# One more buffer for high halves, a gather of unsplit tokens, and the transposition of up behind both down products, in a two-layer decoder kernel

## Chip, cores, metric

One core of a Trainium2 chip runs the whole kernel. The metric is the device time of the kernel in microseconds; the kernel before takes 1362.1 us (median of three runs, 1359.48 to 1362.96).

## What is computed

A decoder trunk of two layers over 256 tokens of 1024 channels in float32. Layer 0 mixes by pooling and sliding-window attention, then a dense SwiGLU; layer 1 mixes by dilated attention and a short convolution, then a SwiGLU of eight experts, of which each token uses two. The change touches the last part:

```python
def swiglu(x, w_gate, w_up, w_down):
    return (jax.nn.silu(x @ w_gate) * (x @ w_up)) @ w_down

def moe_swiglu(x, w_router, w_gate, w_up, w_down):
    top_logit, top_e = lax.top_k((xt @ w_router).astype(jnp.float32), TOP_K)   # 2 of 8
    gates = jax.nn.softmax(top_logit, axis=-1)
    ...
    def expert_block(args):
        xb, e = args
        return (jax.nn.silu(xb @ w_gate[e]) * (xb @ w_up[e])) @ w_down[e]
    ...                                   # gather rows by expert, run, add back by gate

# every sub-layer: x = layer_norm(ALPHA * x + f(x)); expert hidden width 3584
```

## The kernel before

**Weights.** All weights come as one stream of pieces of 1 MB (128 partitions x 2048 float32), loaded by the queue of SyncE (SP) into raw buffers as these come free. Most products are made from float32 split in two: a high half `wh`, cast by ScalarE (ACT, `hi`, L258), and a low half `wl`, what is left after taking `wh` from the raw piece, by VectorE (DVE, `lo`, L275); `lo` then gives the raw buffer back, and with that the next load starts. `wh` has a ring of four tiles, `wl` one of three. When TensorE (PE) has used a piece, `drop` (L301) calls `pump` (L282), which lets ScalarE cast a piece if it is at most two ahead of the piece in use, and VectorE subtract one if it is at most one ahead.

**Experts.** Each expert's hidden width of 3584 is cut into seven chunks of 512. A step (`step`, L1407) does one chunk of one expert: two pieces of gate, two of up, and then the two down pieces of the chunk of the step before it. There are 56 steps. An expert with many tokens is heavy (H): its products take three split matmuls each (`mm3`, L316 to L318), and the two down pieces of most heavy chunks are used raw, as native float32 (L1224). An expert with at most 64 tokens is light (T): it holds the high and low halves of its tokens side by side in 128 columns, so two split matmuls do (`mm2`, L1226 with `wh`, L1227 with `wl`), and the two halves of the result in `h` are transposed and folded together: `fold_of` (L1234) gives four transposes on PE (L1237), a copy of one half on ScalarE (L1240) and an addition of the other on VectorE (L1241). That is done for gate (`sg`) and for up (`us`); afterwards VectorE multiplies them (L1466), ScalarE casts the high half `hh` of the product (L1467), and VectorE subtracts the low one (L1468). `h` is copied from PSUM by ScalarE for gate (L1427) and for up (L1439). The sequence of H and T, by `mixed`, is mostly "heavy, light, light", with some "heavy, light".

**Tokens.** Before an expert starts, its tokens are gathered by products with one-hot matrices (`Unit`, L1161). For that the normalized tokens `x` are split once into `xkh` and `xkl`; `gather` (L1176) multiplies either half, and the copies out of PSUM (`half` L1185, `thin` L1190) go to ScalarE but one. Expert outputs are added into `x` (L1285).

**Order.** The program is written under a manual schedule: each engine runs its instructions in the order in which the code issues them. So the order of `pump`, copies, folds and gathers on ScalarE and VectorE is that of the calls in `step`.

Of the kernel before, what the change touches and what calls it, by code (L numbers as in the profile page):

```python
# [10 lines left out]
F32 = mybir.dt.float32  # L11
F32R = mybir.dt.float32r
# [75 lines left out]
def trunk(ctx, tc, stream, x_tok, x_t, pos, ln_w, ln_b, pool_bd, pool_sc, sinks, conv_w, router, cf, cb, windows,  # L88
# [20 lines left out]
    def bank():  # L109
        return rings.next("bank") if "bank" in rings.at else ps1.tile([128, 512], F32, name="bank")  # L110
# [16 lines left out]
    def split(hi, lo, src):  # L127
        nc.scalar.copy(hi, src)
        nc.vector.tensor_sub(lo, src, hi.bitcast(F32))
# [23 lines left out]
    class Weights:  # L153
        def __init__(self):
            self.order = []
            self.native, self.base = set(), [0]
            self.raw, self.split, self.loaded = {}, {}, 0
            self.free = [raw1.tile([128, PIECE], F32, name=f"raw{i}") for i in range(RAW1)]
            self.kept = {}
            self.limit = LIMIT  # L160
            self.taken = self.used = 0
            self.at_hi = self.at_lo = (0, 0)
# [118 lines left out]

        def pump(self, n=1, full=False):  # L282
            for _ in range(n):
                self.hi(AHEAD if full else AHEAD - 1)
                k = self.at_lo[0]
                if k - self.used < AHEAD - 1 if k >= MOE_BASE else self.step(self.at_lo) != self.at_hi:
                    self.lo()
# [599 lines left out]
    with tc.tile_pool(name="od1", bufs=1) as e1, tc.tile_pool(name="od2", bufs=2) as e2:  # L887
# [151 lines left out]
    identb = cbf[:, B_ID:B_TRI]  # L1039
    early.close()  # L1040
    raw3 = ctx.enter_context(tc.tile_pool(name="raw3", bufs=1))
    xk, yb = [raw2.tile([128, PIECE], F32R, name=f"xk{i}") for i in range(2)], \
        raw2.tile([128, PIECE], F32R, name="yb")
    raws = [raw3.tile([128, PIECE], F32, name=f"raw{RAW1 + i}") for i in range(RAW2 + RAW3 - 3)]
    lasting = raws[:3]
    W.give_back(*raws)
    mm, na, nb, oa, ob = proj_out(wb, lambda: None)
    ctx.enter_context(tc.manual_schedule())
    xkh, xkl = [t.rearrange("p (i d) -> p i d", i=2) for t in xk]
    lgp = bank()  # L1050
    lg0 = lgp[:, :2 * NE].rearrange("p (i e) -> p i e", e=NE)

    def route(norm, c):
# [8 lines left out]
            for k in range(2):  # L1062
                nc.tensor.matmul(lg0[:, i], xt[:, k], rw[:, c + k], start=c + k == 0, stop=c + k == KC - 1)
        return logits

    def split_tokens(i):
        split(xkh[:, i], xkl[:, i], x[:, i])

    na.add(1, oa[1])
    na.finish()  # L1070
# [15 lines left out]
    W.drop(0)  # L1086
    lga()
    lga = route(na, 4)
    nc.scalar.copy(xkh[:, 0], x[:, 0])
    lgb()  # L1090
    nc.vector.tensor_sub(xkl[:, 0], x[:, 0], xkh[:, 0].bitcast(F32))
    lgb = route(na, 6)
    W.lo()
    mm(ob, 3, 1)
# [17 lines left out]
    lga()  # L1112
    lgb()
    keep(KEEP[2])
    nc.scalar.copy(xkh[:, 1], x[:, 1])
    W.hi()
    W.hi()

# [42 lines left out]
    class Unit:  # L1161
# [11 lines left out]
            for i in range(2):  # L1173
                self.one_hot(self.oh[:, i], iota[:, :self.oh.shape[2]], i)

        def gather(self, a, c, b, m):  # L1176
            for k in range(c, c + 512 // m):
                for i in range(2):
                    nc.tensor.matmul(b[:, (k - c) * m:(k - c + 1) * m],  # L1179
                                     (xkh, xkl)[a][:, i, k * 128:(k + 1) * 128],  # L1180
                                     self.oh[:, i], start=i == 0, stop=i == 1)

        def half(self, c, a, b, copy):
            self.gather(a, c, b, 128)
            copy(self.xg[a][:, c:c + 4], b.rearrange("p (k s) -> p k s", s=128))  # L1185

        def thin(self, a):
            b = bank()
            self.gather(a, 0, b, LIGHT)
            nc.scalar.copy(self.xg[0][:, :, a * LIGHT:(a + 1) * LIGHT], b.rearrange("p (k s) -> p k s", s=LIGHT))  # L1190

        def parts(self):
            yield self.start()
            for j in range(2 if self.light else 4):
                if self.light:
                    self.thin(j)
                else:
                    self.half(4 * (j % 2), j // 2, bank(), nc.vector.tensor_copy if j == 3 else nc.scalar.copy)
                yield

        def aim(self):
            ohb = rings.tiles["ohb"][0]
# [86 lines left out]
    nc.vector.tensor_copy(cnt, psb[:, 16:24])  # L1289
    ln2.close()  # L1290
    m2 = ctx.enter_context(tc.tile_pool(name="mo2", bufs=1, side="right"))
    rings.add("oh", [m2.tile([128, 2, 128], F32R, name="oh")])
    rings.add("ohb", [m2.tile([128, 2, 128], F32R, name="ohb")])
    rings.add("oht", [m2.tile([128, 2, 128], F32R, name="oht")])
    rings.add("h", [m2.tile([128, 512], F32, name="h")])
# [5 lines left out]
    accs = [acc() for _ in range(4)]  # L1301
    rings.add("bank", [bank() for _ in range(4)])
    places = [big_tile(t) for t in ("mh", "ml")]
    unit = Unit(places[0], 0, False, slot)
    unit.start()
    nc.vector.tensor_sub(xkl[:, 1], x[:, 1], xkh[:, 1].bitcast(F32))
    W.lo()
    for c in (0, 4):
        unit.half(c, 0, acc(), nc.scalar.copy)
    for c in (0, 4):  # L1310
        unit.half(c, 1, bank(), nc.vector.tensor_copy if c == 0 else nc.scalar.copy)
    for _ in range(4):
        W.hi()
    W.lo()
# [4 lines left out]
    def gates():  # L1319
        nc.vector.tensor_scalar(gt[:, 0], gt[:, 1], 1.0, None, op0=OP.add)  # L1320
        nc.vector.reciprocal(gt[:, 0], gt[:, 0])
        nc.vector.tensor_mul(gt[:, 1], gt[:, 1], gt[:, 0])
        nc.vector.tensor_mul(gate, hots[0], bc(gt[:, 0]))
        nc.vector.tensor_mul(hots[1], hots[1], bc(gt[:, 1]))
        nc.vector.tensor_add(gate, gate, hots[1])
        nc.scalar.activation(x, x, AF.Copy, scale=ALPHA)

    def sort_experts():
        rank = cst[:, C_RANK:C_INV]
# [39 lines left out]
    class Experts:  # L1369
# [37 lines left out]
        def step(self, s):  # L1407
            nonlocal aux, ones_row, rows, wb
            p, n = self.seq[s]
            unit, left = self.units[p], len(self.seq) - 1 - s  # L1410
            light = unit.light
            self.part(p)
            ended = self.units[self.prev[0]] if self.prev is not None and self.prev[1] == NCH - 1 else None
            if ended or left == 0:
                (ended or unit).aim()

            def proj(b, j):
                (half_light if light else half_proj)(b, W.take(512), j, *unit.xg)
# [12 lines left out]
            up = bank()  # L1431
            proj(up, 0)
            if light:
                sg, us = rings.next("sg"), rings.next("us")
                fold_of(sg, h)()
                nc.scalar.activation(sg, sg, AF.Silu)
            proj(up, 1)
            if light:
                nc.scalar.copy(h, up)  # L1439
            else:  # L1440
                nc.vector.tensor_mul(h, h, up)
            self.part()
            if left < 4:
                spread(*divmod(3 - left, 2))
            if self.prev is not None:
                pe, pn, pht = self.prev
                if pn == 0:
                    self.begin(pe)
                finish(down_half(self.y[pe], pht, 0, pn, W.take(None)))
                W.drop()  # L1450
            if light:
                fold_up = fold_of(us, h)
            if left == 0:
                unit.back()
            if self.prev is not None:
                finish(down_half(self.y[pe], pht, 1, pn, W.take(None)))
                W.drop()
                if ended:
                    split_y(yb[:, :D], yb[:, D:], self.y.pop(pe))
                    ended.back()  # L1460
                    self.todo = combine_of(pe, ended.oht)
            if light:
                ht = rings.next("hh")
                s3 = sg.rearrange("p (k t) -> p k t", t=LIGHT)
                fold_up()
                nc.vector.tensor_mul(sg, sg, us)  # L1466
                nc.scalar.copy(ht[:, :, :LIGHT], s3)  # L1467
                self.late = lambda: nc.vector.tensor_sub(ht[:, :, LIGHT:], s3, ht[:, :, :LIGHT].bitcast(F32))  # L1468
                self.prev = (p, n, (ht,))
            else:  # L1470
                self.prev = (p, n, flip_h(h, (p, n, 4) in self.native))
            if s >= FIXED:
                self.follow(p, n)
            if left == 6:
                aux = W.borrow(0)
                ones_row = aux[:1, :128]
                nc.vector.memset(ones_row, 1.0)
                rows = W.borrow(1)[:1].rearrange("p (a d) -> p a d", a=2)
                for a, src in enumerate((ln_w, ln_b)):
                    nc.sync.dma_start(rows[:, a], src[1, 1][None, :])  # L1480
                wb = W.borrow(2).rearrange("p (a d) -> p a d", a=2)
            if left == 9:
                W.hold(*lasting)
# [23 lines left out]
    def tail(x8):  # L1507
# [2 lines left out]
        x8.settle()  # L1510
        spare = bank()
        for _ in range(7):
            nc.tensor.matmul(spare, xkh[:, 0, :128], xkh[:, 0, :512], start=True, stop=True)
        e, n, ht = x8.prev
        y, oht = x8.y[e], x8.units[e].oht

# [205 lines left out]
```

## Time and profile before

| | |
|---|---|
| median of three runs | 1362.1 us (1359.48 to 1362.96) |
| the profiled execution, its own time | 1365.56 us |
| its span in the trace | 1363.8 us, at a granted TensorE clock of 0.99 |
| busy in the span | PE 97%, weight loads 78%, VectorE 80%, ScalarE 67%, GpSimd 0% |
| HBM traffic | 424.88 MB read, 1.05 MB written |

The profiled execution is 3.5 us longer than the median; the rows below are of that one. Times in the trace are microseconds from the span's start. The first 475 us or so hold layer 0 and the mixer and router of layer 1, the rest is the expert part with a tail of some 20 us. In a row of the trace "x8" counts records; a native float32 matmul leaves two records, and the listing of instructions below counts it once.

### The profile page before, as it was taken

Reading aid. Unit: us, or ns where it says so; the run is one execution under the profiler, and the core shown is the slowest. Engines: PE = TensorE matmul, PEld = TensorE weight load, DVE = VectorE, ACT = ScalarE, POOL = GpSimd, SP = SyncE. Lnnn points to the kernel's source line nnn. Section 1 sums busy time; section 2 is a strip of 40 time slices with the busy share of each in tenths; the row PEclk is TensorE's granted clock in tenths of the full one; section 3 lists DMA queues with packets and bytes.
Section 4 is the critical chain, followed back from the end, with each engine's and each line's share of the span. In section 5 each row is a group of like instructions: output and inputs, shape, how many; then the busy total and the mean of one; then the engine's idle time right before and its main releaser. Section 6 shows DMA issues by size and latency. Waiting matters only on the chain. (4 is left out here: it accounts for less than half of the span.)

```text
span 1363.8 us, 18760 instructions
## 1 busy us (share of the span) xinstructions
PE 1321.2 (97%) x6944; PEld 1069.5 (78%) x6944; DVE 1084.4 (80%) x1110; ACT 917.3 (67%) x1026; POOL 2.5 (0%) x8
## 2 busy tenths in 40 slices
PE   8999999999999989999999999999999999999995
PEld 6888999988999778877777777787777877777764
DVE  6866555587655688899898899898889979988987
ACT  5735444455544477788776788778678769776883
POOL 0000000000000000000000000000000000000000
PEclk9999999999999999999999999999999999999998
DMA  8617655535424689999999999999999999999991
GB/s 261 234 62 222 205 187 186 187 124 186 155 78 149 261 307 370 346 417 401 420 387 362 377 420 420 418 419 419 419 392 419 419 405 419 420 419 350 418 411 41
DMA packets 72375, 426.61 MB, mean 313 GB/s; under 512 B 8914, under 2 KB 9682, under 8 KB 30548
## 3 DMA queue, kind: packets, MB, share of 16 engines
q1 hardware_dynamic: 71412, 424.32, 79.9%
q0 software_dynamic: 576, 0.62, 0.3%
q8 instruction: 56, 0.92, 0.3%
q10 hardware_dynamic: 288, 0.39, 0.1%
q14 instruction: 43, 0.35, 0.1%
HBM read 424.88 MB, written 1.05 MB: 312 GB/s over the span
## 5 line engine op out<-in xcount | busy, mean ns | idle before, releaser
L275 DVE TENSOR_TENSOR wl<-raw,wh 128x2048 fp32r<-128x2048 f32 (+2 forms) x435 | 823.6, 1914 | 155.6 <-ACT wh L258 126.9
L258 ACT CAST wh<-raw 128x2048 fp32r<-128x2048 f32 (+2 forms) x437 | 695.0, 1607 | 140.1 <-PE bank L318 62.8
L1226 PE MATMUL bank<-wh,ml 128*128 128x512 f32 x536 | 220.5, 411 | 1.1 <-ACT h L1427 1.1
L1227 PE MATMUL bank<-wl,ml 128*128 128x512 f32 x536 | 211.5, 395 | 0.9 <-DVE wl L275 0.6
L318 PE MATMUL bank<-wl,mh 128*128 128x512 f32 x336 | 131.8, 392 | 3.1 <-DVE wl L275 3.1
L316 PE MATMUL bank<-wh,mh 128*128 128x512 f32 x336 | 134.0, 399 | 0.0
L317 PE MATMUL bank<-wh,mh 128*128 128x512 f32 x336 | 131.4, 391 | 0.4 <-ACT mh L1185 0.4
L1227 PEld LDWEIGHTS bank<-wl,ml 128*128 128x128 f32 x536 | 100.8, 188 | 28.5 <-DVE wl L275 6.1
L1226 PEld LDWEIGHTS bank<-wh,ml 128*128 128x128 f32 x536 | 100.8, 188 | 22.6 <-issue 3.1
L316 PE MATMUL bank<-xth,wh 128*128 128x256 f32 x416 | 118.1, 284 | 0.0
L317 PE MATMUL bank<-xth,wl 128*128 128x256 f32 x416 | 117.7, 283 | 0.0
L318 PE MATMUL bank<-xtl,wh 128*128 128x256 f32 x416 | 117.7, 283 | 0.0
L1226 PE MATMUL acc<-wh,hh 128*128 128x512 f32 (+1 forms) x308 | 115.3, 381 | 0.8 <-DVE hh L1468 0.8
L1224 PE MATMUL acc<-raw,hf 128*128 128x512 f32 x256 | 115.2, 593 | 0.0
L1227 PE MATMUL acc<-wl,hh 128*128 128x512 f32 (+1 forms) x308 | 112.9, 373 | 0.0
L1224 PEld LDWEIGHTS acc<-raw,hf 128*128 128x128 f32 x256 | 47.1, 190 | 47.1 <-issue 46.0
L316 PEld LDWEIGHTS bank<-xth,wh 128*128 128x128 f32 x416 | 79.8, 192 | 0.4
L317 PEld LDWEIGHTS bank<-xth,wl 128*128 128x128 f32 x416 | 79.8, 192 | 0.4
L318 PEld LDWEIGHTS bank<-xtl,wh 128*128 128x128 f32 x416 | 79.8, 192 | 0.0
L318 PEld LDWEIGHTS bank<-wl,mh 128*128 128x128 f32 x336 | 63.5, 189 | 16.9 <-DVE wl L275 3.5
L317 PEld LDWEIGHTS bank<-wh,mh 128*128 128x128 f32 x336 | 63.5, 189 | 14.6 <-issue 1.0
L316 PEld LDWEIGHTS bank<-wh,mh 128*128 128x128 f32 x336 | 63.5, 189 | 13.8 <-issue 1.0
(284 smaller groups left out, 1849.0 us busy)
## 6 DMA issues: line engine op xcount, KB each, us to landing
raw<-in_stream SPq DMA_DIRECT2D x326, 1024.0 KB, 9.8
raw<-in_stream SPq DMA_DIRECT2D x142, 512.0 KB, 4.9
ln_wb<-in_ln_w SPq DMA_DIRECT2D x3, 512.0 KB, 8.1
ln_wb<-in_ln_b SPq DMA_DIRECT2D x3, 512.0 KB, 9.5
xraw<-in_x_t SPq DMA_DIRECT2D x4, 256.0 KB, 7.2
raw<-in_stream SPq DMA_DIRECT2D x4, 256.0 KB, 5.0
x<-in_x_tok SPq DMA_DIRECT2D x1, 1024.0 KB, 7.0
win<-in_windows SPq DMA_DIRECT2D x1, 768.0 KB, 10.9
```

Of the source, the lines that this page charges most:

```text
L258: nc.scalar.copy(self.split[k][0][:, c], self.raw[k][:, c])
L275: nc.vector.tensor_sub(wl[:, c], self.raw[k][:, c], wh[:, c].bitcast(F32))
L316: nc.tensor.matmul(o, ah, bh, start=start, stop=False)
L317: nc.tensor.matmul(o, al, bh, start=False, stop=False)
L318: nc.tensor.matmul(o, ah, bl, start=False, stop=stop)
L1224: nc.tensor.matmul(o, a if a.dtype == F32 else a.bitcast(F32), bh, start=start, stop=stop)
L1226: nc.tensor.matmul(o, a, bh, start=start, stop=False)
L1227: nc.tensor.matmul(o, a, bl, start=False, stop=stop)
```

## The change

It has three parts.

1. The ring of `wh` gets a fifth tile, and from then on `pump` lets ScalarE cast up to three pieces ahead of the one in use (`W.deep = AHEAD`), where it was two. The rule for `lo` is as before.
2. The tokens are no longer split. `x` stays as `tokens`, sums go into a new tile `xsum`, the one-hot matrix is float32, and `gather` multiplies the unsplit tokens by native matmuls: 16 per unit where there were 32. The result is split out of PSUM by `split`: ScalarE casts the high half, VectorE subtracts.
3. `fold_of(us, h)`, the transposition of up and its copy, is called behind both down halves instead of between them.

```diff
@@ pump
-                self.hi(AHEAD if full else AHEAD - 1)
+                self.hi(AHEAD if full else self.deep)
@@ after the early pools are closed
-    xk, yb = [raw2.tile([128, PIECE], F32R, name=f"xk{i}") for i in range(2)], \
-        raw2.tile([128, PIECE], F32R, name="yb")
+    xsum = raw2.tile([128, 2, D], F32, name="xsum")
+    yb = raw2.tile([128, PIECE], F32R, name="yb")
+    rings.tiles["wh"].append(raw2.tile([128, PIECE], F32R, name=f"wh{AHEAD + 1}"))
+    W.deep = AHEAD
...
-    nc.scalar.copy(xkh[:, 0], x[:, 0])
-    nc.vector.tensor_sub(xkl[:, 0], x[:, 0], xkh[:, 0].bitcast(F32))
...
@@ Unit
-        def gather(self, a, c, b, m):
-            for k in range(c, c + 512 // m):
+        def gather(self, c, b):
+            m = LIGHT if self.light else 128
+            for k in range(512 // m):
                 for i in range(2):
-                    nc.tensor.matmul(b[:, (k - c) * m:(k - c + 1) * m],
-                                     (xkh, xkl)[a][:, i, k * 128:(k + 1) * 128],
+                    nc.tensor.matmul(b[:, k * m:(k + 1) * m], tokens[:, i, (c + k) * 128:(c + k + 1) * 128],
                                      self.oh[:, i], start=i == 0, stop=i == 1)
...
+            hi, lo = [t[:, c:c + 512 // m] for t in self.xg] if not self.light else \
+                     [self.xg[0][:, :, a * m:(a + 1) * m] for a in range(2)]
+            split(hi, lo, b.rearrange("p (k s) -> p k s", s=m))
...
@@ before the experts
+    tokens, x = x, xsum
...
-        nc.scalar.activation(x, x, AF.Copy, scale=ALPHA)
+        nc.scalar.activation(x, tokens, AF.Copy, scale=ALPHA)
@@ step
                 finish(down_half(self.y[pe], pht, 0, pn, W.take(None)))
                 W.drop()
-            if light:
-                fold_up = fold_of(us, h)
             if left == 0:
                 unit.back()
             if self.prev is not None:
                 finish(down_half(self.y[pe], pht, 1, pn, W.take(None)))
                 W.drop()
...
             if light:
+                fold_up = fold_of(us, h)
                 ht = rings.next("hh")
                 s3 = sg.rearrange("p (k t) -> p k t", t=LIGHT)
                 fold_up()
```

The change moves lines: L1224 becomes L1209, L1226 and L1227 become L1211 and L1212, L1237, L1240 and L1241 become L1222, L1225 and L1226; L1427, L1439, L1466 and L1467 become L1410, L1422, L1448 and L1449.

How PE's rows change in a light step behind a heavy one, in the stretch from the end of up to the next gate (`hf` is the heavy chunk's product, `ml` the tokens of the light expert). Before:

```order
L1226 MATMUL bank<-wh_80,ml 128x512
L1227 MATMUL bank<-wl_84,ml 128x512
L1224 MATMUL acc<-raw_4332,hf 128x512 x4
L1237 MATMUL bank<-cst,h 128x128 x4
L1224 MATMUL acc<-raw_4333,hf 128x512 x4
L1226 MATMUL bank<-wh_81,ml 128x512
L1227 MATMUL bank<-wl_85,ml 128x512
```

Now:

```order
L1211 MATMUL bank<-wh_80,ml 128x512
L1212 MATMUL bank<-wl_84,ml 128x512
L1209 MATMUL acc<-raw_4332,hf 128x512 x4
L1209 MATMUL acc<-raw_4333,hf 128x512 x4
L1222 MATMUL bank<-cst,h 128x128 x4
L1211 MATMUL bank<-wh_81,ml 128x512
L1212 MATMUL bank<-wl_85,ml 128x512
```

The four transposes of `h` have gone from between the two native down halves to behind the second.

ScalarE's rows for the same step, from the copy of the heavy product (`hf`) to the cast of the light product (`hh`). Before:

```order
L1249 COPY hf<-bank 128x512
L258 CAST wh_80<-raw_4330 128x2048
L1427 COPY h<-bank 128x512
L1240 COPY sg<-bank 128x256
L1436 ACTIVATE sg<-sg 128x256
L258 CAST wh_81<-raw_4331 128x2048
L1439 COPY h<-bank 128x512
L258 CAST wh_82<-raw_4335 128x2048
L1240 COPY us<-bank 128x256
L258 CAST wh_79<-raw_4336 128x2048
L1467 CAST hh<-sg 128x4x64
```

Now:

```order
L1234 COPY hf<-bank 128x512
L1410 COPY h<-bank 128x512
L258 CAST wh_81<-raw_4331 128x2048
L1225 COPY sg<-bank 128x256
L1419 ACTIVATE sg<-sg 128x256
L258 CAST wh_82<-raw_4335 128x2048
L1422 COPY h<-bank 128x512
L258 CAST wh_4329<-raw_4336 128x2048
L258 CAST wh_79<-raw_87 128x2048
L1225 COPY us<-bank 128x256
L1449 CAST hh<-sg 128x4x64
```

Each cast of a piece stands about one place earlier against the copies of `h` and the folds, and the copy of `us` stands directly ahead of `hh`.

VectorE's rows in the like step of an earlier expert, from the fold of gate (`sg`) to the low half of the light product. Before:

```order
L1241 TENSOR_TENSOR sg<-sg,bank 128x256
L275 TENSOR_TENSOR wl_85<-raw,wh_79 128x2048
L275 TENSOR_TENSOR wl_83<-raw_4330,wh_80 128x2048
L1241 TENSOR_TENSOR us<-us,bank 128x256
L1466 TENSOR_TENSOR sg<-sg,us 128x256
L1169 TENSOR_SCALAR ohb<-iota,hot_4610 128x128 x2
L275 TENSOR_TENSOR wl_84<-raw_4332,wh_81 128x2048
L1468 TENSOR_TENSOR hh<-sg,hh 128x4x64
```

Now:

```order
L1226 TENSOR_TENSOR sg<-sg,bank 128x256
L275 TENSOR_TENSOR wl_85<-raw,wh_79 128x2048
L275 TENSOR_TENSOR wl_83<-raw_4330,wh_80 128x2048
L1226 TENSOR_TENSOR us<-us,bank 128x256
L1448 TENSOR_TENSOR sg<-sg,us 128x256
L1164 TENSOR_SCALAR ohb<-iota,hot_4607 128x128 x2
L275 TENSOR_TENSOR wl_84<-raw_4332,wh_81 128x2048
L1450 TENSOR_TENSOR hh<-sg,hh 128x4x64
```

VectorE's order is the same before and now.

## Rows read from the trace of the kernel before

**Rows 1.** The page: busy time, and DMA in 40 slices (tenths).

```profile
PE 1321.2 (97%) x6944; PEld 1069.5 (78%) x6944; DVE 1084.4 (80%) x1110; ACT 917.3 (67%) x1026; POOL 2.5 (0%) x8
...
DMA  8617655535424689999999999999999999999991
```

**Rows 2.** Busy time by stretch: engines' busy us (instructions), PE clock, DMA share, GB/s.

```profile
740.00:1220.00 480.00, 478.16 (x2086) 361.43 (x2085) 426.22 (x295) 377.74 (x329) 0.00 (x0) 1.00 1.00 413
```

**Rows 3.** Waits, 580 to 1340 us: us in total, times, longest us.

```profile
DVE wl L275 <- ACT wh L258: 40.8, 27, 2.3
...
PE bank L1237 <- ACT h L1439: 2.8, 4, 1.4
...
PE bank L1227 <- DVE wl L275: 0.6, 2, 0.3
...
PEld bank L1227 <- DVE wl L275: 6.1, 15, 0.7
```

**Rows 4.** Timeline of VectorE, 1128 to 1177: start, us, what [idle before, releaser].

```profile
1131.21 0.41 DVE L1241 TENSOR_TENSOR us<-us,bank 128x256 f32<-128x256 f32 x1
...
1156.92 8.89 DVE L275 TENSOR_TENSOR wl<-raw,wh 128x2048 fp32r<-128x2048 f32 x4
1166.44 0.42 DVE L1241 TENSOR_TENSOR sg<-sg,bank 128x256 f32<-128x256 f32 x1 [0.64 <-ACT sg L1240]
1169.13 4.58 DVE L275 TENSOR_TENSOR wl<-raw,wh 128x2048 fp32r<-128x2048 f32 x2 [2.27 <-ACT wh L258]
1173.63 0.41 DVE L1241 TENSOR_TENSOR us<-us,bank 128x256 f32<-128x256 f32 x1
```

**Rows 5.** Timeline of PE, 1161 to 1180.

```profile
1163.12 0.39 PE L1227 MATMUL bank<-wl,ml 128*128 128x512 f32 x1
1163.35 0.39 PE L1226 MATMUL bank<-wh,ml 128*128 128x512 f32 x1
1163.66 0.50 PE L1227 MATMUL bank<-wl,ml 128*128 128x512 f32 x1
...
1167.68 3.60 PE L1224 MATMUL acc<-raw,hf 128*128 128x512 f32 x8
1171.12 0.60 PE L1237 MATMUL bank<-cst,h 128*128 128x128 f32 x4
1171.55 3.60 PE L1224 MATMUL acc<-raw,hf 128*128 128x512 f32 x8
1174.59 0.80 PE L1226 MATMUL bank<-wh,ml 128*128 128x512 f32 x1
```

**Rows 6.** Timeline of ScalarE, 1161 to 1177.

```profile
1166.03 0.37 ACT L1240 COPY sg<-bank 128x256 f32<-128x256 f32 x1 [1.89 <-PE bank L1237]
...
1171.75 0.37 ACT L1240 COPY us<-bank 128x256 f32<-128x256 f32 x1 [0.37 <-PE bank L1237]
```

**Rows 7.** Busy time in the cycle of one heavy and two light steps.

```profile
1131.21:1163.60 32.39, 32.32 (x145) 25.70 (x143) 32.17 (x23) 28.01 (x24) 0.00 (x0) 1.00 1.01 420
...
1131.21:1173.63 42.42, 42.35 (x181) 31.89 (x180) 39.29 (x27) 35.29 (x31) 0.00 (x0) 1.00 1.01 420
```

**Rows 8.** Timeline of VectorE, 634 to 668 and, in a heavy step, 850 to 884.

```profile
636.00 0.41 DVE L1241 TENSOR_TENSOR us<-us,bank 128x256 f32<-128x256 f32 x1
...
856.56 2.29 DVE L275 TENSOR_TENSOR wl<-raw,wh 128x2048 fp32r<-128x2048 f32 x1 [0.95 <-issue]
```

**Rows 9.** Gathers and native matmuls: timelines of PE, and L129 by line (count, busy us, mean ns).

```profile
585.65 1.87 PE L1179 MATMUL bank<-oh,xk 128*128 128x64 f32 x16
...
416.26 1.00 PE L1013 MATMUL bank<-v,pt 128*128 128x64 f32 x8
...
L129 DVE TENSOR_TENSOR yb<-acc,yb 128x512 fp32r<-128x512 f32 x14 | 9.3, 687 | 7.6 <-ACT yb L128 7.6
```

**Rows 10.** Timelines of VectorE and PE at the first gather.

```profile
470.55 1.22 DVE L1306 TENSOR_TENSOR xk<-x,xk 128x1024 fp32r<-128x1024 f32 x1
...
470.54 2.10 PE L1179 MATMUL acc<-oh,xk 128*128 128x128 f32 x16 [0.69 <-PE bank L1151]
```

More of the change, by code (lines that the diff above doesn't have):

```diff
@@ L158, in __init__ @@
             self.free = [raw1.tile([128, PIECE], F32, name=f"raw{i}") for i in range(RAW1)]
[L159 removed]
+            self.kept, self.deep = {}, AHEAD - 1
             self.limit = LIMIT
@@ L1048, in trunk @@
     ctx.enter_context(tc.manual_schedule())
-    xkh, xkl = [t.rearrange("p (i d) -> p i d", i=2) for t in xk]
     lgp = bank()
@@ L1064, in route @@
         return logits
-    def split_tokens(i):
-        split(xkh[:, i], xkl[:, i], x[:, i])
     na.add(1, oa[1])
@@ L1114, in trunk @@
     keep(KEEP[2])
-    nc.scalar.copy(xkh[:, 1], x[:, 1])
     W.hi()
@@ L1174, in start @@
                 self.one_hot(self.oh[:, i], iota[:, :self.oh.shape[2]], i)
-        def gather(self, a, c, b, m):
-            for k in range(c, c + 512 // m):
+        def gather(self, c, b):
+            m = LIGHT if self.light else 128
+            for k in range(512 // m):
                 for i in range(2):
-                    nc.tensor.matmul(b[:, (k - c) * m:(k - c + 1) * m],
-                                     (xkh, xkl)[a][:, i, k * 128:(k + 1) * 128],
+                    nc.tensor.matmul(b[:, k * m:(k + 1) * m], tokens[:, i, (c + k) * 128:(c + k + 1) * 128],
                                      self.oh[:, i], start=i == 0, stop=i == 1)
[L1183 to L1190, printed above, removed]
+            hi, lo = [t[:, c:c + 512 // m] for t in self.xg] if not self.light else \
+                     [self.xg[0][:, :, a * m:(a + 1) * m] for a in range(2)]
+            split(hi, lo, b.rearrange("p (k s) -> p k s", s=m))
         def parts(self):
             yield self.start()
[L1194 to L1199, printed above, removed]
+            for c in (0,) if self.light else (0, 4):
+                yield self.gather(c, bank())
         def aim(self):
@@ L1291, in trunk @@
     m2 = ctx.enter_context(tc.tile_pool(name="mo2", bufs=1, side="right"))
-    rings.add("oh", [m2.tile([128, 2, 128], F32R, name="oh")])
+    rings.add("oh", [m2.tile([128, 2, 128], F32, name="oh")])
     rings.add("ohb", [m2.tile([128, 2, 128], F32R, name="ohb")])
@@ L1303, in trunk @@
     places = [big_tile(t) for t in ("mh", "ml")]
+    tokens, x = x, xsum
     unit = Unit(places[0], 0, False, slot)
     unit.start()
-    nc.vector.tensor_sub(xkl[:, 1], x[:, 1], xkh[:, 1].bitcast(F32))
     W.lo()
     for c in (0, 4):
-        unit.half(c, 0, acc(), nc.scalar.copy)
-    for c in (0, 4):
-        unit.half(c, 1, bank(), nc.vector.tensor_copy if c == 0 else nc.scalar.copy)
+        unit.gather(c, bank())
     for _ in range(4):
@@ L1512, in tail @@
         for _ in range(7):
-            nc.tensor.matmul(spare, xkh[:, 0, :128], xkh[:, 0, :512], start=True, stop=True)
+            nc.tensor.matmul(spare, places[1][:, :128], places[1][:, :512], start=True, stop=True)
         e, n, ht = x8.prev
```

## The prediction, made before the changed kernel was run

> **What bounds the kernel now.** I read the page first, then busy time by stretch, then waits by engine, then single instructions of three engines around one place. The page shows TensorE busy for 97% of the span, and the DMA engines at nine tenths or more in nearly every slice from the sixteenth on [rows 1]. The expert part runs from about 475 to 1345 us. In its middle, 740 to 1220, PE is busy 478.16 of 480.00 us, VectorE 426.22, ScalarE 377.74 [rows 2]. So an edit there cannot win much by feeding PE better; it can lose by making PE wait. By waits, PE lost 2.8 us to folds behind the `h` copy and 0.6 us to low halves (`wl`) between 580 and 1340; the weight loads beside it waited 6.1 us for low halves. VectorE waited 40.8 us, 27 times, for high halves (`wh`) [rows 3]. That last number is what the fifth buffer can remove, and the question is whether it costs anything today.
>
> It does not, but VectorE is nearer to being the pace than its share says. Take a light step whose down products belong to the heavy step before it (I call it HT), at 1160 to 1175. VectorE adds the fold of up at 1131.21 (L1241) and again at 1173.63, one heavy and two light steps later: a cycle of 42.42 us. From 1131.21 on it works without a gap worth naming until 1165.81, when the run of four `wl` that began at 1156.92 ends; only then come the waits of 0.64 and 2.27 us [rows 4]. Up to 1163.60, where the third of the four ends, VectorE is busy 32.17 of 32.39 us [rows 7]. PE needs that third `wl` at once: its matmuls follow each other every 0.23 us (1163.12 to 1163.35), but between 1163.35 and 1163.66 there are 0.31, because L1227 had to wait for it [rows 5]. So the order is: add of up, 32.4 us of VectorE without slack, `wl` of the first up half, PE at 1163.66, both down products, next add of up. PE is busy 42.35 of 42.42 us in this cycle [rows 7] and yet waits for VectorE by a hair: the two are level.
>
> **The change part by part.** *The fold of up moves behind both downs.* Before, PE runs the first native down from 1167.68, the four transposes from 1171.12, the second down from 1171.55, and the next gate at 1174.59 [rows 5]. The copy of the fold starts at 1171.75, 0.63 after the transposes [rows 6], but the add waits on VectorE's own two `wl` until 1173.63 [rows 4]. Afterwards the transposes follow the second down: not before 1174.16 (1174.59 less the 0.43 they take) and not after 1174.56 (1171.12 plus 3.44, the first down's time). The copy follows 0.63 later, the add 0.41 after the copy's start (as from 1166.03 to 1166.44 in the fold of the gate [rows 4, 6]): 1175.20 to 1175.60, so 1.57 to 1.97 later than 1173.63. I take 1.8. VectorE's order of instructions is unchanged, so everything behind the add, starting with a `wl`, is 1.8 later too; nothing in the 32.4 us that follow can give it back, and PE waits 1.8 at the next HT. A cycle whose only slack is 0.05 us grows by 1.8. I find seven such cycle ends in the trace, the first add at 636.00, the last at 1173.63 [rows 4, 8]: 7 x 1.8 = +12.6. There are sixteen HT steps with native downs. In the other nine VectorE waits later in the cycle; before the `wl` at 856.56, for example, 4 us behind such an add, it idles 0.95 us [rows 8], and there the shift is absorbed at least in part. Bounds: 0 if PE's queue absorbs all of it, 16 x 1.97 = +31.5 if all sixteen pay.
>
> *The fifth buffer.* With casts three pieces ahead the `wh` at 1169.13 is there when VectorE is free at 1166.86, so its two `wl` end at 1171.4 instead of 1173.7. That would help only if the add could follow; it now waits for the fold until about 1175.4, and the 2.27 us of idle become 4.0. Elsewhere it removes at most what PE and its loads waited for low halves, 0.6 and 6.1 us [rows 3]. I take -1, bounds -6.7 and 0, since the loads overlap matmuls. The casts themselves are the same in number; one more stands ahead of the copies of `h` and the folds on ScalarE in places, which has 102 us of 480 free [rows 2].
>
> *Waits of the fold behind the `h` copy.* PE lost 2.8 us to them [rows 3]; behind two downs the copy is always done. I take -2, bounds -2.8 and 0.
>
> *The native gather on PE.* Sixteen split matmuls of 64 columns took 1.87 us, so the 32 of one unit 3.74 [rows 9]. Afterwards there are 16 native ones. The order has four L1224 where the trace counts eight [rows 5], so a native matmul is two records; L1013, native with 64 columns too, took 1.00 us for 8 records, 0.25 for one matmul [rows 9], which makes 4.0 per unit. That is +0.26 for each of eight units (five light, three heavy), +2 at most; with 0 as the other end I take +1. The first of them, at 470.54, stands in PE's way alone, the subtraction of 1.22 us on VectorE that is dropped beside it at 470.55 does not [rows 10]: nothing there.
>
> The Trainium skill says in "FP8 and Floating Point Precision", section TensorE Precision Notes, that a true FP32 product takes four passes through the array. The wide native product agrees: 3.44 us for four matmuls is 0.86 each, 3.7 times the 0.23 between split ones of the same width; the narrow L1013 does not, being 2.1 times 0.117.
>
> *The gather's split.* A unit's low half is now a subtraction on VectorE, 0.69 us by the like L129 [rows 9]: one for each of five light units, one net for each of two later heavy ones, 4.8 in all, and in front of it VectorE may wait for ScalarE's copy, as that waits for PE's burst. ScalarE saves one copy of 0.59 per light unit. This hides where VectorE idles 2.27 us anyway and counts where it paces: bounds 0 and +5, I take +2.
>
> *Sum.* 12.6 - 1 - 2 + 1 + 2 = +12.6. The profiled execution took 1365.56 us, which makes 1378.2; it lies 3.5 above the median of 1362.1, so the forecast is 1374.7, **1375 us**.
>
> **The rivals.** *Faster: the buffer beats the move.* If PE alone is the pace, as its 42.35 of 42.42 us allow, and the 0.31 us at 1163.66 are an accident of the weight load, then VectorE's 2.27 us gained and 1.8 us lost cancel, and PE gets back the waits: 2.8, 0.6 and up to 6.1 us, against +1 for the gather. That is -8.5: 1353 to 1354. For it: 40.8 us of waits on `wh`, 27 of them and up to 2.3 us long. Against it: they all stand behind the point at which PE waited. It decides if the cycle at HT stays at 42.4 or below.
>
> The Trainium skill, in "Perfetto Trace Analysis", section Optimization Strategy, reads a gap that keeps repeating on the engine that should be saturated as a possible sign of too few buffers. By that rule the 27 gaps are what the fifth buffer cures, and the time is this rival's. The gaps are on VectorE here, not on PE, and the rows above bear it out only in part; I give it its chance of 0.18.
>
> *No change: the shift mostly hidden.* If only two or three of the seven cycles pass it on (+3.6 to +5.4) and the small gains come in, the sum is about 0 to +2: 1362 to 1364. For it: a slack of a few tenths in a cycle, or `wl` that finish earlier once ScalarE's casts lie elsewhere, would be enough in some. Chance 0.17.
>
> *Much slower: every HT pays.* The nine cycles with slack have it only because VectorE is in time there; with the subtractions of the gather and a late add it may be gone. Then 16 x 1.8 = 28.8, and 1391. Chance 0.06.
>
> *The gather is dear.* If a native matmul of 64 or 128 columns cost 3.7 split ones, as the wide one does, a unit would take 16 x 3.7 x 0.117 = 6.9 us, 3.2 more than now; eight units +25 in place of +1, and 1399. L1013 speaks against it. Chance 0.03.
>
> **How the numbers follow.** The forecast (five to nine cycles pay, +9 to +16, with the small terms nearer one end or the other: 1367 to 1384) has 0.56, the faster rival 0.18, no change 0.17, the two slower ones 0.09. A measurement of this kernel tells about 0.3% from no change, 4.1 us: faster is below 1358.0, slower above 1366.2. Faster 0.18, same 0.17, slower 0.56 + 0.06 + 0.03 = 0.65. For 8 in 10 the range must take in the forecast and no change (0.73) and part of both ends: 1355 on the left, 1391 on the right. Cases of both signs do not share the most of it; the forecast's own range is 1367 to 1384.
>
> **What would show it.** Right: at the HT steps the fold of up stands some 3 us later on PE than between the downs; VectorE waits for `us` from ScalarE about 4 us there, where before it waited 2.27 for `wh`; the cycle of one heavy and two light steps is 44.2 us instead of 42.4 in about seven places; and PE shows new waits at L1212 (the former L1227) for `wl`, 10 us or more together. Wrong: PE's waits between 580 and 1340 fall, or the cycles keep their 42.4 us, which would mean that VectorE had slack that I did not see; or the time grows at the gathers, where then one burst of 16 matmuls would be well over 4 us.

## The result: 1373.2 us, slower by 0.9%, and the profile after

The changed kernel takes 1373.21 us in the median (1370.92 to 1378.39) against 1362.1: a ratio of 1.0088, interval 1.0065 to 1.011. The forecast was 1375, a ratio of 1.0095 to the same median.

The page of the changed kernel, in its first rows: span, busy time, and DMA in 40 slices.

```profile
span 1371.4 us, 18687 instructions
...
PE 1325.8 (97%) x6944; PEld 1066.0 (78%) x6944; DVE 1081.9 (79%) x1116; ACT 907.6 (66%) x1016; POOL 2.5 (0%) x8
...
DMA  8616655536425689999999999999999999998991
```

Beside [rows 1] nothing seems to have happened: PE is still at 97%, VectorE and ScalarE have a little less to do. The stretch [rows 2] tells more. PE, PEld, VectorE and ScalarE from 740 to 1220, as in those rows:

```profile
740.00:1220.00 480.00, 472.19 (x2041) 351.88 (x2040) 417.56 (x289) 363.17 (x319) 0.00 (x0) 1.00 0.99 406
```

PE was busy 478.16 of 480 us and is 472.19 now, with 2041 instead of 2086 matmul records: the same program runs through this stretch more slowly, and no engine works more. So something waits. Waits of the changed kernel from 580 to 1340 us (us in total, times, longest), answering to [rows 3]:

```profile
DVE us L1226 <- ACT us L1225: 60.1, 17, 4.2
...
PE acc L1212 <- DVE wl L275: 3.9, 10, 0.4
PE bank L1222 <- ACT h L1410: 3.4, 8, 0.5
PE bank L1212 <- DVE wl L275: 1.7, 3, 0.7
...
PEld bank L1212 <- DVE wl L275: 14.3, 29, 1.2
PEld acc L1212 <- DVE wl L275: 9.9, 14, 0.8
```

VectorE's 40.8 us of waits for high halves are gone altogether: the fifth buffer does what it was put there for. In their place stand 60.1 us of waits for `us`, the late fold's copy, and PE now waits for low halves (5.6 us in place of 0.6, its weight loads 24.2 in place of 6.1).

One such place, the same step as in [rows 4 to 6], first VectorE, then PE, then ScalarE of the changed kernel:

```profile
1137.62 0.42 DVE L1226 TENSOR_TENSOR us<-us,bank 128x256 f32<-128x256 f32 x1 [4.11 <-ACT us L1225]
...
1172.48 0.42 DVE L1226 TENSOR_TENSOR sg<-sg,bank 128x256 f32<-128x256 f32 x1 [0.62 <-ACT sg L1225]
1172.82 4.65 DVE L275 TENSOR_TENSOR wl<-raw,wh 128x2048 fp32r<-128x2048 f32 x2
1181.64 0.42 DVE L1226 TENSOR_TENSOR us<-us,bank 128x256 f32<-128x256 f32 x1 [4.17 <-ACT us L1225]
```

```profile
1180.60 0.60 PE L1222 MATMUL bank<-cst,h 128*128 128x128 f32 x4
```

```profile
1175.52 3.70 ACT L258 CAST wh<-raw 128x2048 fp32r<-128x2048 f32 x2
1181.24 0.37 ACT L1225 COPY us<-bank 128x256 f32<-128x256 f32 x1 [2.02 <-PE bank L1222]
```

The two `wl` at 1172.82 follow the addition of gate with no wait (it was 2.27 us), and are done by 1177.5. Then VectorE has nothing that it may do: next in its order is the addition of up, its copy waits on ScalarE for transposes that stand behind 6.9 us of native down products, and 4.17 us pass. The cycle from addition to addition is 44.02 us, 42.42 before.

```profile
1137.62:1181.64 44.02, 43.01 (x182) 31.70 (x181) 39.03 (x25) 34.94 (x30) 0.00 (x0) 1.00 1.01 420
```

Where PE pays for it: in this cycle its starts show four new gaps. At 1143.09 the fold of gate waits for a copy of `h` (it starts 0.82 us after the matmul before in place of 0.23), at 1148.03 and twice more (at 1167.51 and 1169.71, 0.48 us in place of 0.23) a `wl` is late.

```profile
1143.09 0.66 PE L1222 MATMUL bank<-cst,h 128*128 128x128 f32 x4 [0.44 <-ACT h L1410]
...
1147.27 0.39 PE L1211 MATMUL acc<-wh,hh 128*128 128x512 f32 x1
1148.03 0.50 PE L1212 MATMUL acc<-wl,hh 128*128 128x512 f32 x1 [0.38 <-DVE wl L275]
```

From 1147.27 to 1148.03 there are 0.76 us where 0.23 is usual: half a microsecond for one `wl`. The four gaps make 1.6 us, by which the cycle grew; 0.6 of that is a wait for ScalarE, which stands in order behind the late transposes too (2.02 us in the row of 1181.24).

**What the two profiled executions differ in otherwise.** The changed one is its kernel's median, the one of before lies 3.5 us above its own. Its early part was slow for another reason, seen in the granted clock (last three columns: clock, DMA share, GB/s). Before:

```profile
329.50:332.00 2.50, 2.50 (x7) 1.94 (x6) 0.42 (x1) 0.77 (x2) 0.00 (x0) 0.50 0.74 205
466.00:469.00 3.00, 3.00 (x12) 1.49 (x11) 1.96 (x12) 2.24 (x4) 0.00 (x0) 0.56 0.00 0
```

After, the same instructions:

```profile
328.20:331.00 2.80, 2.80 (x15) 2.32 (x13) 0.67 (x2) 1.35 (x4) 0.00 (x0) 1.00 0.85 275
463.00:466.00 3.00, 3.00 (x23) 1.68 (x22) 2.31 (x14) 1.43 (x3) 0.00 (x0) 1.00 0.00 0
```

So the expert part must be compared by itself. From the first gather to the end it took 1363.8 - 470.54 = 893.3 us before and 1371.4 - 466.69 = 904.7 after: 11.4 more, near what the medians say (11.1). One more stretch at the lower clock, of before alone, lies inside that part, at about 698; it comes up again with the gather.

### The profile page after: what moved, and what is told of

Its sections match the earlier page's. It is cut to its first block, busy times and chain, and to the rows that moved or that the text cites. A ratio compares the mean times of both kernels' runs of the same rounds, so it can differ in the third digit from the quotient of the medians.

```text
span 1371.4 us, 18687 instructions
## 1 busy us (share of the span) xinstructions
PE 1325.8 (97%) x6944; PEld 1066.0 (78%) x6944; DVE 1081.9 (79%) x1116; ACT 907.6 (66%) x1016; POOL 2.5 (0%) x8
## 4 chain that ended last, share of the span: by engine, by line
PE 80%; DVE 13%; ACT 4%; DMA 2%; issue 2%; SPq 0%; DVEq 0%; ACTq 0%
PE bank L318 9%; PE bank L317 9%; PE bank L316 9%; DVE wl L275 9%; PE acc L1209 8%; PE bank L1212 7%; PE bank L1211 6%; PE acc L318 4%; PE acc L317 4%; PE acc L316 4%; PE acc L1212 4%; PE acc L1211 3%; PE bank L1175 2%; ACT wh L258 2%; DMA raw<-in_stream 2%; PE bank L1222 2%
## 5 line engine op out<-in xcount | busy, mean ns | idle before, releaser
L1211 PE MATMUL bank<-wh,ml 128*128 128x512 f32 x536 | 218.2, 407 | 0.0
L1212 PE MATMUL bank<-wl,ml 128*128 128x512 f32 x536 | 213.4, 398 | 3.7 <-DVE wl L275 2.1
L1212 PEld LDWEIGHTS bank<-wl,ml 128*128 128x128 f32 x536 | 100.7, 188 | 35.8 <-DVE wl L275 15.1
L1212 PE MATMUL acc<-wl,hh 128*128 128x512 f32 (+1 forms) x308 | 113.6, 376 | 4.2 <-DVE wl L275 3.9
L1211 PEld LDWEIGHTS bank<-wh,ml 128*128 128x128 f32 x536 | 100.9, 188 | 18.1 <-issue 1.2
L1211 PE MATMUL acc<-wh,hh 128*128 128x512 f32 (+1 forms) x308 | 113.1, 374 | 1.5 <-DVE hh L1450 1.5
L1209 PE MATMUL acc<-raw,hf 128*128 128x512 f32 x256 | 112.4, 592 | 0.0
L1209 PEld LDWEIGHTS acc<-raw,hf 128*128 128x128 f32 x256 | 48.4, 190 | 54.7 <-issue 52.9
L1212 PEld LDWEIGHTS acc<-wl,hh 128*128 128x128 f32 x308 | 58.0, 188 | 20.1 <-DVE wl L275 9.9
L317 PEld LDWEIGHTS bank<-wh,mh 128*128 128x128 f32 x336 | 63.6, 189 | 12.8
```

Source lines behind the costliest of these rows:

```text
L317: nc.tensor.matmul(o, al, bh, start=False, stop=False)
L1209: nc.tensor.matmul(o, a if a.dtype == F32 else a.bitcast(F32), bh, start=start, stop=stop)
L1211: nc.tensor.matmul(o, a, bh, start=start, stop=False)
L1212: nc.tensor.matmul(o, a, bl, start=False, stop=stop)
```

## Experiments

All ratios are to the kernel before, run on the same chip beside the variant; every interval is one of 95%. Its median was 1363.4 us beside groups 1 and the first run of 2, 1362.7 beside 3 and 4, and 1361.7 beside the second run of 2 and 5.

**1. Each part by itself.** First the changed kernel with the fold of up back between the down products:

```diff
                 finish(down_half(self.y[pe], pht, 0, pn, W.take(None)))
                 W.drop()
+            if light:
+                fold_up = fold_of(us, h)
...
             if light:
-                fold_up = fold_of(us, h)
                 ht = rings.next("hh")
```

> The changed kernel with the fold of up back between the two down products; the fifth buffer and the native gather stay. Theory (the late fold delays VectorE's addition at light steps behind heavy ones, and VectorE paces there): the addition follows the transposes again, and since the high halves are ready the two subtractions ahead of it no longer wait 2.27 us, so the cycle of one heavy and two light steps falls from 44.0 us to PE's own 41.9 or so: 1352 to 1360 us. Rival (the gather's subtraction or the crowded ScalarE queue of the fifth buffer costs the time): it stays at 1368 to 1374. Rival (the fifth buffer is worth nothing): 1362, like the kernel before.

Measured: 1356.7 us, ratio 0.9952 (0.9931 to 0.9972). Moving these lines alone turns a loss of 0.9% into a gain of 0.5%. VectorE's additions of up in that run:

```profile
1126.14 0.42 DVE L1226 TENSOR_TENSOR us<-us,bank 128x256 f32<-128x256 f32 x1 [0.68 <-ACT us L1225]
...
1131.02 4.49 DVE L275 TENSOR_TENSOR wl<-raw,wh 128x2048 fp32r<-128x2048 f32 x2 [1.46 <-PE bank L1212]
...
1168.38 0.42 DVE L1226 TENSOR_TENSOR us<-us,bank 128x256 f32<-128x256 f32 x1 [0.73 <-ACT us L1225]
```

It waits 0.7 us in place of 4.2, and just behind, at 1131.02, it now waits 1.46 us for PE to give a buffer of low halves back: it is ahead of PE. The cycle is 42.24 us; PE is busy for 42.17 of it. The expectation had 41.9 for PE's own pace; little is left to gain from VectorE here.

Then the kernel before with the opposite edit alone, the fold of up behind both down products:

> The kernel before with nothing changed but the fold of up behind both down products: four buffers, split tokens. Theory: the addition of up comes 1.8 us later in each light step behind a heavy one whatever the buffers are, and about eight cycles pass it on; PE saves some 2 us at folds: 1370 to 1377 us. Rival (the slowdown needs the fifth buffer, whose casts stand ahead of the copy of up on ScalarE): 1360 to 1364. Rival (the native gather is the cost): 1360 to 1364 too.

Measured: 1380.5 us, ratio 1.0128 (1.0097 to 1.016), so +17 us: more than the whole change, and above the expected range. Two rivals fall (that it needs the fifth buffer, that the gather costs the time). Its waits on VectorE:

```profile
DVE wl L275 <- ACT wh L258: 39.1, 23, 2.4
DVE us L1241 <- ACT us L1240: 30.5, 18, 2.2
```

Both waits stand there at once, here at the step of [rows 4]:

```profile
1180.28 4.58 DVE L275 TENSOR_TENSOR wl<-raw,wh 128x2048 fp32r<-128x2048 f32 x2 [2.27 <-ACT wh L258]
1186.74 0.42 DVE L1241 TENSOR_TENSOR us<-us,bank 128x256 f32<-128x256 f32 x1 [1.89 <-ACT us L1240]
```

2.27 and 1.89 are together the changed kernel's 4.2. The cycle is 44.14 us.

Last, the native gather alone: the changed kernel with the fold between the down products and without the fifth tile.

```diff
-    rings.tiles["wh"].append(raw2.tile([128, PIECE], F32R, name=f"wh{AHEAD + 1}"))
-    W.deep = AHEAD
```

> The changed kernel with the fold of up between the down products and without the fifth buffer (casts two pieces ahead as before): what is left is the native gather of unsplit tokens alone. Theory: +1 on PE and 0 to +5 on VectorE, 1362 to 1367 us. Rival (the gather is the cost of the change): 1370 to 1375. The difference to the run with the fold between the down products and the fifth buffer is what the buffer is worth.

Measured: 1361.3 us, ratio 0.998 (0.9963 to 0.9996): a gain of 2 to 3 us where I had expected a loss of 0 to 5. VectorE still waits 31.7 us for high halves here, and not at all in the first run of this group, which is 4.6 us faster by the medians (3.6 by the means, give or take 2.0): that is what the fifth buffer is worth when the fold stands between.

**2. Which steps pay.** The fold between the down products only in light steps behind heavy ones, and the mirror of it:

```diff
+            after_heavy = self.prev is not None and not self.units[self.prev[0]].light
+            if light and after_heavy:
+                fold_up = fold_of(us, h)
...
             if light:
-                fold_up = fold_of(us, h)
+                if not after_heavy:
+                    fold_up = fold_of(us, h)
```

> The changed kernel with the fold of up between the down products only in light steps that follow a heavy one (native down products, 3.44 us each); behind both in light steps that follow a light one. Theory (only the former pay): within 3 us of the run with all folds between the down products, 1352 to 1361 us. Rival (the late fold costs in every light step, each by the length of one down product): half or more of the loss stays, 1364 to 1372.

Measured: 1358.3 us, ratio 0.9968 (0.9952 to 0.9983).

> The mirror of the run with the fold between the down products behind heavy steps only: here it stands behind both down products in light steps that follow a heavy one, and between them in those that follow a light one; fifth buffer and native gather as in the changed kernel. Theory: nearly the whole loss is back, 1369 to 1376 us, with VectorE waiting about 4 us for the copy of up in each such step. Rival (the loss needs both kinds of steps, so that each half costs half): 1362 to 1367.

Measured: 1372.0 us, ratio 1.008 (1.0065 to 1.0095). Nearly all of the loss is in the steps behind heavy ones, as expected; having the fold behind a light step's split down products costs 1.6 us by the medians, which the spread of the runs does not tell from nothing. VectorE's waits for the fold's copy, the mirror first, then the other:

```profile
DVE us L1226 <- ACT us L1225: 53.2, 15, 4.2
```

```profile
DVE us L1226 <- ACT us L1225: 16.0, 16, 2.3
```

The mirror shows something that the expectation did not have: how PE pays. Its waits there, 580 to 1340 us:

```profile
PE bank L1222 <- ACT h L1422: 12.2, 11, 1.2
PE bank L1222 <- ACT h L1410: 4.0, 9, 0.5
PE bank L1212 <- DVE wl L275: 1.0, 2, 0.7
```

PE hardly waits for low halves, and its weight loads wait 6.5 us for them, about as in the first run of group 1 (6.0). It waits at the folds for ScalarE's copies of `h`, 16.2 us in all against 2.9 there. In the cycle from 1139.54 to 1183.46 (43.92 us) the only two such waits of PE are 0.44 us for the copy of gate and 1.15 for that of up. ScalarE's order holds the copy of `us`, the cast of `hh`, casts of pieces and the next copy of `h`, so the late transposes hold back that copy as they hold back VectorE's subtractions; with the folds behind light steps left between the down products, PE meets the copy first.

**3. Is it the order on VectorE, or the late transposes themselves?** Here PE's order is the changed kernel's, both downs ahead of the fold. Behind heavy steps, but for the last nine of the 56 steps, only the addition, the product and its cast move: they are issued after the first piece of the next step, by when VectorE has been given one more subtraction.

```diff
@@ settle
-                self.late()
-                self.late = None
+                late, self.late = self.late, None
+                late()
@@ step
-                fold_up()
-                nc.vector.tensor_mul(sg, sg, us)
-                nc.scalar.copy(ht[:, :, :LIGHT], s3)
-                self.late = lambda: nc.vector.tensor_sub(ht[:, :, LIGHT:], s3, ht[:, :, :LIGHT].bitcast(F32))
+                def merge():
+                    fold_up()
+                    nc.vector.tensor_mul(sg, sg, us)
+                    nc.scalar.copy(ht[:, :, :LIGHT], s3)
+                    self.late = lambda: nc.vector.tensor_sub(ht[:, :, LIGHT:], s3, ht[:, :, :LIGHT].bitcast(F32))
+
+                if self.prev is not None and not self.units[self.prev[0]].light and left > 8:
+                    self.late = merge
+                else:
+                    merge()
```

> The changed kernel, TensorE's order untouched (fold of up behind both down products), but in light steps behind heavy ones VectorE adds the fold, multiplies, and ScalarE casts the product only after the first piece of the next step is done, so that VectorE has one more subtraction (three, not two) ahead of the addition. Theory (the loss is VectorE idling about 4 us in order behind a late fold, not the fold's place on TensorE): the idle time takes up a subtraction of 2.2 us, the cycle of one heavy and two light steps falls below 43 us, 1354 to 1363 us. Rival (the late transposes themselves cost, on TensorE or through the bank or h that they hold): 1368 to 1374. Rival (the product comes too late for the down products): 1368 and more, with waits of TensorE on hh.

Measured: 1363.2 us, ratio 0.9998 (0.9977 to 1.0019), at the upper end of the range and a hair beyond it. VectorE at the like step:

```profile
1163.68 6.93 DVE L275 TENSOR_TENSOR wl<-raw,wh 128x2048 fp32r<-128x2048 f32 x3
1172.48 0.42 DVE L1226 TENSOR_TENSOR us<-us,bank 128x256 f32<-128x256 f32 x1 [1.87 <-ACT us L1225]
```

Three `wl` instead of two stand ahead of the addition, 1.87 us of waiting are left of 4.17, and the cycle is 42.78 us. With PE's order unchanged, 10 us of the loss are gone; so most of it comes from what stands in order behind the late addition, and not from the place of the transposes on PE. Whether that is VectorE's subtractions or ScalarE's copies this run does not tell, since the cast of `hh` on ScalarE moves with the addition; the mirror in group 2 shows that PE can pay nearly all of it through ScalarE's. Some 6.5 us to the first run of group 1 remain. The seven cycles that grew in the changed kernel (see below) are 0.2 to 0.7 us longer here than there, 3.4 together; the rest was not taken apart.

**4. How deep, and which ring.** With the fold between the down products: casts four pieces ahead with five buffers, and three ahead with four.

```diff
-    W.deep = AHEAD
+    W.deep = AHEAD + 1
```

> Fold of up between the down products, native gather, five buffers of high halves, casts up to four pieces ahead instead of three. Theory (with three ahead VectorE no longer waits for high halves, so more depth has nothing to give): within 3 us of the run with three ahead, 1354 to 1360 us. Rival (ScalarE's casts then stand in front of the copies that TensorE and VectorE wait for): 1362 to 1372.

Measured: 1376.0 us, ratio 1.0097 (1.0078 to 1.0116): the rival, and 4 us beyond its range.

```diff
-    rings.tiles["wh"].append(raw2.tile([128, PIECE], F32R, name=f"wh{AHEAD + 1}"))
```

> Fold of up between the down products, native gather, casts three pieces ahead, but only the four buffers of before. Theory (the fifth buffer is needed because a cast that reuses a buffer just used waits in ScalarE's order): VectorE and TensorE wait behind ScalarE a little, 1358 to 1366 us. Rival (the order of the casts, not the buffer, is what gains): 1354 to 1358, like the run with five.

Measured: 1376.8 us, ratio 1.0102 (1.0084 to 1.012): worse than either expectation. Both let ScalarE ask for every buffer of the ring. Waits with four ahead on ScalarE and PE:

```profile
ACT wh L258 <- PE bank L317: 47.0, 50, 3.5
ACT wh L258 <- PE bank L1211: 24.7, 10, 2.6
...
PE bank L1222 <- ACT h L1422: 11.6, 12, 1.1
PE bank L1222 <- ACT h L1410: 5.7, 11, 0.8
```

A cast waits on PE for a buffer that PE has just finished, and the copies of `h` queue behind it on ScalarE; PE's folds then wait for the copies, 17.3 us in all where the run with three ahead has 2.9 (16.3 with three ahead in four tiles). So the gain of the fifth tile is a cast one piece earlier that still finds a free buffer; depth up to the last buffer loses more than that.

Then the fifth tile for low halves, with the fold behind both downs:

```diff
-    rings.tiles["wh"].append(raw2.tile([128, PIECE], F32R, name=f"wh{AHEAD + 1}"))
-    W.deep = AHEAD
+    rings.tiles["wl"].append(raw2.tile([128, PIECE], F32R, name=f"wl{AHEAD}"))
...
-                if k - self.used < AHEAD - 1 if k >= MOE_BASE else self.step(self.at_lo) != self.at_hi:
+                if k - self.used < AHEAD if k >= MOE_BASE else self.step(self.at_lo) != self.at_hi:
```

> The changed kernel with the fifth tile given to the low halves instead of the high ones: casts two pieces ahead as before, subtractions up to two pieces ahead (one before), fold of up behind both down products. Theory: VectorE gets a third subtraction ahead of the addition, so the late fold costs little; but each subtraction now follows its cast closely and may wait for it: 1356 to 1368 us. Rival (only the depth of the casts helps): like the run of the fold move alone, 1374 to 1382.

Measured: 1453.6 us, ratio 1.0674 (1.0651 to 1.0696), a miss of both. VectorE's subtraction now comes directly behind the cast of the same piece in the program, and 60 of the 236 subtractions from 580 to 1340 us wait for it (27 waits in the kernel before):

```profile
DVE wl L275 <- ACT wh L258: 128.7, 60, 2.3
```

What else stands in VectorE's order (`h`, `sg`) is late with it, and ScalarE and PE wait in turn (PE 19.2 us for low halves, 24.1 for copies of `h`). In this kernel the subtractions had better stay a piece behind the casts.

**5. A version that beats both.** The fold between all down products was run a second time beside a variant that keeps it behind the light ones but defers its addition there as in 3.

> The changed kernel with every fold of up between the down products, a second time, as a measure for the two beside it: 1355 to 1359 us.

Measured: 1355.7 us, ratio 0.9963 (0.9946 to 0.9979).

> The fold of up between the down products behind heavy steps; behind both down products after light steps, and there VectorE adds it only after the first piece of the next step, so that no subtraction waits for it. Theory (TensorE's waits for the copy of up go, about 2 us, and VectorE loses nothing): 1353 to 1357 us. Rival (TensorE is bound anyway, or the late product makes the down products wait): 1356 to 1362.

Measured: 1357.4 us, ratio 0.9971 (0.9957 to 0.9986), a little above the range, as the rival has it, and not to be told from the run beside it. The best found is the change without its third part: five buffers, native gather, fold of up between the down products, 5 to 7 us below the kernel before.

## Why the prediction was right, and where its terms were off

**The place and the first half of the mechanism** were right. The addition of up came 1.6 us later in the cycle shown (44.02 against 42.42; the forecast said 1.8 and 44.2), VectorE waits 4.2 us where about 4 were forecast, and the waits for high halves turned into waits for the fold. Runs of groups 1 to 3 say the same from three sides: the fold's place, the kind of step, the order behind the addition. The second half, that the delay reaches PE through VectorE's low halves, was only partly right: the forecast had VectorE and PE level and left out ScalarE, which stands in order behind the same transposes. In the cycle shown 1.0 of the 1.6 us reach PE through low halves and 0.6 through a copy of `h`; in the mirror of group 2, which is nearly as slow, nearly all goes through copies of `h`. (The slack of 0.05 us that the forecast gave the cycle is 0.07 by [rows 7]; nothing hangs on it.)

**The count** was right by number, not by place, and so in part by luck. The sixteen additions behind heavy steps make fifteen cycles; in the two traces seven of them grew by 1.4 to 1.6 us, 10.8 together (12.6 forecast). The one from 767.42 is typical:

```profile
767.42 0.41 DVE L1241 TENSOR_TENSOR us<-us,bank 128x256 f32<-128x256 f32 x1
```

It lasts until the addition at 809.81, 42.39 us; after, from 765.29 to 809.26, 43.97:

```profile
765.29 0.42 DVE L1226 TENSOR_TENSOR us<-us,bank 128x256 f32<-128x256 f32 x1 [4.16 <-ACT us L1225]
...
809.26 0.42 DVE L1226 TENSOR_TENSOR us<-us,bank 128x256 f32<-128x256 f32 x1 [4.13 <-ACT us L1225]
```

But the cycle from 636.00, which I had counted, grew by 0.1 only, like one other of my seven; in both a heavy expert's gather begins, and they did not grow with the move alone either. Why was not taken apart. Two that I had left out as having slack (from 882.26 and 1052.69) grew by 1.4. Of the other six, one grew by 0.8 and one by 0.4, two stayed, and two shrank, by 1.7 where the gather lies that is shown below and by 2.3 at the last. I had taken any idle time of VectorE behind the addition for slack; it is slack only where PE does not need what comes next.

**Where PE pays** was half wrong. The forecast had 10 us or more of waits on L1212; there are 5.6 on the matmuls, 24.2 on their weight loads, and another 3.4 where the fold of gate waits for the copy of `h` (L1410), a wait that was 0.5 before. The 2.8 us behind the other copy of `h` did vanish, as I had it, and these came in their place: the gain of -2 that I booked was taken back at the next fold. The run with the fold alone shows the same 3.4, so it comes with the move, not with the buffer.

**The terms.** The move and the buffer were too small in my sum, and the gather had the wrong sign. Fold: 12.6 - 2 = 10.6 forecast, 17.1 measured alone (interval 13 to 22). Gather: +1 and +2 forecast, about -2.7 measured (0.998 of 1363). Fifth buffer: -1 forecast, -4.6 measured with the fold between. The three measured alone add up to 9.8, the whole change to 11.1, the forecast to 12.6: the errors cancel, and that the time came out so near is in part luck.

The gather's error has a row. Before, the four bursts of a heavy expert's gather lay between other work, and one of them waited:

```profile
695.35 1.11 PE L1179 MATMUL bank<-oh,xk 128*128 128x128 f32 x8 [2.11 <-ACT h L1439]
```

The changed kernel has two bursts of 16 records and no such wait, and with the gather alone the additions of up at 682.46 and 733.87, between which this lies, are 3.4 us closer together (those before them 0.9 further apart); I had costed instructions only. Part of the 3.4 is the clock. Behind that wait the matmuls of before start 0.42 us apart in place of 0.23, at a granted clock of 0.50 from 698 to 700, which makes about 1.5 us by these rows:

```profile
697.70 0.63 PE L1227 MATMUL acc<-wl,hh 128*128 128x512 f32 x1
698.12 0.63 PE L1226 MATMUL acc<-wh,hh 128*128 128x512 f32 x1
```

The run with the fold move alone, which has the split gather too, shows the same pair there, a wait of 2.13 us and a granted clock of 0.50 from 696 to 698. The runs with the native gather, but for the one of 1453.6 us, show no such stretch from 510 to 1330 us. So the native gather seems to win by a wait of PE and a fall of the clock that it avoids; that the one causes the other was not tried. For the narrow matmuls themselves the bound of 0 was the right one: 16 native ones of 64 columns took as long as 32 split ones (3.74 us).

```profile
581.80 3.68 PE L1175 MATMUL bank<-oh,x 128*128 128x64 f32 x32
```

That is 0.23 us each, twice a split one, where the four passes that the Trainium skill gives for true FP32 ("FP8 and Floating Point Precision", TensorE Precision Notes) would make 0.47, by an estimate from [rows 9] (4 x 0.117); the wide native product agrees (3.7 times a split one), the narrow one shows no more than two split ones' time.

**The rivals.** That the buffer wins did not happen to the change, but it was right about the buffer: with the fold put back, 1356.7 us, near the 1353 to 1354 it had. What the Trainium skill says on repeating gaps ("Perfetto Trace Analysis", Optimization Strategy) fits that far: with the fold between the down products, one more buffer removed all 31.7 us of them, and that was worth some 4 us, since most of them were not on the path.

## What to carry to other kernels

An engine that runs in program order is delayed by the latest of its inputs, so before you move a producer behind a long piece of work on another engine, look at what stands behind its consumer, not at the consumer: here a 0.4 us addition, and the copy and cast beside it, held back subtractions and copies for which PE waited 5 to 32 us later. When a ring gets one more buffer, leave one free in the look-ahead; an engine that asks for the last one waits in order, with everything behind it. And run the parts of a change alone: a sum that comes out right can hide one part that loses more than the whole and two that gain.

## What the runs showed of the hardware that was not expected

In the profiled execution of before, TensorE's granted clock was 0.50 from 329.5 to 332 us and 0.56 from 466 to 469, that is mostly the level of 1.2 GHz, while the same instructions ran at 1.00 in the changed kernel's execution. Ahead of the first, PE had sat idle for 2.90 us on a copy, in the other execution for 2.27:

```profile
327.17 0.71 PE L385 MATMUL bank<-cst,ks 128*128 128x128 f32 x4 [2.90 <-ACT kth L387]
```

```profile
326.53 0.71 PE L385 MATMUL bank<-cst,ks 128*128 128x128 f32 x4 [2.27 <-ACT kth L387]
```

That the longer wait caused it was not tried, and the length of this wait alone does not decide: the execution of the run with the fold between the down products behind heavy steps only waited 3.26 us there and stayed at 1.00. By the first gather the execution of before was 3.9 us behind the other: 0.6 by the longer wait, 1.6 by the lower clock behind it, and 1.6 at the second place. It lay 3.5 us above its median.
